# A list schedule with new latencies and port costs, helper work ranked by latest begin, and a look ahead

## The chip, the cores and the metric

The kernel runs on one core of a Trainium2 chip, as one launch. The time is device microseconds of that core. Five queues of instructions run beside each other, each in its own order: PE (TensorE, matmuls and transposes), DVE (VectorE), ACT (ScalarE), POOL (GpSimd) and SP (SyncE, which issues every DMA here). Work that isn't PE's is called helper work below.

## The reference, cut to what matters

One inference step of a two-layer backbone for 128 context tokens and 512 latent tokens, width 1024. Each layer modulates and normalises its input, projects it once for three attention mixers and for gates, runs the mixers, merges them through sigmoid gates, projects, and then runs a squared-ReLU MLP of width 4096.

```python
for l in range(DEPTH):                      # 2 layers; context and latent tokens alike
    sh1, sc1, g1, sh2, sc2, g2 = split(silu(c) @ w_mod[l] + b_mod[l], 6)
    h = rmsnorm(x, g_pre_mix) * (1 + sc1) + sh1
    qa, ka, va, qbd, kvbd, kbr, qc, kc, vc, gates = split(h @ w_in)
    oa = windowed attention with a sink      # 8 heads of 64, 2 key heads, axial rotary
    ob = latent attention                    # 8 heads, low-rank queries and keys
    oc = attention with normalised q and k   # 8 heads of 64, 2 key heads, axial rotary
    ga, gb, gc = split(sigmoid(gates), 3)
    mixed = (ga * (oa @ w_oa) + gb * (ob @ w_ob) + gc * (oc @ w_oc)) @ w_out
    x = x + g1 * rmsnorm(mixed, g_post_mix)
    h = rmsnorm(x, g_pre_mlp) * (1 + sc2) + sh2
    x = x + g2 * rmsnorm(square(relu(h @ w_mlp1)) @ w_mlp2, g_post_mlp)
```

It returns both outputs and the new keys and values of the context tokens.

## The kernel before

**Precision.** Every float32 operand of a matmul is split in two parts: ACT copies it rounded (`wh`, `ah`, `oh`, `ph`), DVE subtracts that from the original (`wl`, `al`, `ol`, `pl`). `mm3` (line 507) then runs three matmuls in place of one. So each weight costs one DMA into a raw buffer `wr` (three in turn), ACT and DVE work, and three times its matmuls.

**Stages of a layer.** All 640 tokens go through together, in five tiles of 128. First come the projections and the heads of mixer B (`b_proj`, `b_rope`, `b_heads`), then the groups of heads of mixers A and C (`gqa_group`), 100 to 634 us in layer 0 and 1262 to 1803 us in layer 1. For each block of 128 queries PE makes the scores (`sps`), DVE their negative maximum (`nm`), ACT the exponentials (`pt`), DVE the reciprocal of the sum (`rc`), POOL multiplies (`pt`, `normalise`, line 920). PE turns them (`tps`), ACT and DVE split them (`ph`, `pl`), PE multiplies by the values (`ops`). `drive` (line 1808) mixes fill work into these loops: the gates' matmuls (`gate_gen`) and, in layer 0, the modulation vectors (`mod_gen`, line 648), which use DVE, ACT and POOL to add up weighted rows of `w_mod` in `macc`.

Then `merge` (line 1525) loads the heads' outputs back (`orw`), splits them (`oh`, `ol`), multiplies, and scales by the gates (`tg`); `wout` projects into `fps`, and `post` and `norm_mod` add the residual and normalise. The MLP's first half starts with `mlp1_first`, then `sums` (line 1663) makes sums of the inputs (`t0` to `t3`, split in `t0h`, `t0l` and so on), and `mlp1_pair` (line 1698) runs 14 pairs of blocks a layer with seven products in place of eight; POOL makes four sums `s` of the weights `wq` for each pair. The second half is `mlp2_block` and, last, `kblock`.

**The order of the work.** None of these functions issues anything. `Recorder.record` (line 223) notes each operation with what it depends on, `cost` (line 188) guesses how long it holds its engine (`busy`) and when its result is there (`wait`), and `buffers` adds nodes for buffers that are taken and given back. `schedule` (line 335) then runs a list schedule: it always takes the engine that can begin first, and on it the operation with the lowest `prio` of those ready, where `prio` is the place in the program. `emit` issues the operations in the order in which the schedule began them; that is each engine's order on the chip. In `schedule` a result is seen by another engine 0.2 us after its end (`LAT`, line 169), by PE 0.35 us after (`LAT_PE`, line 170); a DVE operation without PSUM operands that begins while any POOL operation runs takes up to 0.6 of the overlap longer; a POOL operation is never slowed; PE always has its full clock. Since `emit` issues everything, the profile puts nearly all instructions at line 461; they are told apart by the tiles that they write and read.

Of the kernel before, what the change touches and what calls it, by code (L numbers as in the profile page):

```python
# [29 lines left out]
QB_SCALE = 96.0 ** -0.5  # L30
LAT = 512

# [118 lines left out]


class Op:
    __slots__ = ("eng", "name", "args", "kw", "prio", "busy", "wait", "preds", "succs", "left", "ready", "start", "end", "dma", "views", "sb", "tokens", "ring")


class Queue:
# [7 lines left out]
class Recorder:  # L165

    LAT = 0.2
    LAT_PE = 0.35  # L170

    def __init__(self, nc):
        self.nc = nc
# [49 lines left out]
    def record(self, eng, name, args, kw):  # L223
        op = Op()
        op.eng, op.name, op.args, op.kw = eng, name, args, kw
        op.prio = len(self.ops) - self.offset
        op.dma = name == "dma_start"
        op.preds, op.succs, op.views, op.tokens, op.ring = {}, [], [], 0, None
        everything = list(enumerate(args)) + list(kw.items())
        outs = [v for k, v in everything if isinstance(v, View) and k in (0, "out", "accum_out")]  # L230
        ins = [v for k, v in everything if isinstance(v, View) and k not in (0, "out", "accum_out")]
        op.views = outs + ins
        op.sb = not any(v.root.space == "PSUM" for v in op.views)
        op.busy, op.wait = self.cost(op, outs, ins)
        if op.dma:
            v = op.views[0]
            op.wait = (v.hi - v.lo) * v.idx.size * 4
        for views, write in ((ins, False), (outs, True)):
            for v in views:
                r, m, keep, seen = v.root, v.mask(), [], False  # L240
                for a in r.acc:
                    o, w, lo, hi, am = a
                    if o is not op and (write or w) and am & m and lo < v.hi and v.lo < hi:
                        seen = True
                        raw = w and not write
                        self.edge(op, o, raw)
# [12 lines left out]
        return op  # L259
# [7 lines left out]
    def node(self):  # L267
        op = Op()
        op.eng, op.preds, op.succs, op.busy, op.wait, op.dma, op.prio, op.views = None, {}, [], 0, 0, False, 0, []
        op.tokens, op.ring = 0, None  # L270
        return op


# [59 lines left out]


    def schedule(self):
        everything = self.ops + self.buffers()
        for o in everything:
            o.left, o.ready = len(o.preds) + o.tokens, 0.0
            for p, data in o.preds.items():
                p.succs.append((o, data))  # L340
        engines = ("tensor", "vector", "scalar", "gpsimd", "sync")
        free = dict.fromkeys(engines, 0.0)
        later = {e: [] for e in engines}
        now = {e: [] for e in engines}
        count = 0
        pool_end, net = 0.0, 0.0

        def less(s, t, todo):
            nonlocal count
            s.ready = max(s.ready, t)  # L350
            s.left -= 1
            if not s.left:
                if s.eng is None:
                    s.start = s.end = s.ready
                    todo.append(s)
                else:
                    count += 1
                    heapq.heappush(later[s.eng], (s.ready, count, s))

        def release(o):  # L360
            todo = [o]
            while todo:
                p = todo.pop()
                if p.ring:
                    takes, bufs, given = p.ring
                    given[0] += 1
                    if bufs + given[0] <= len(takes):
                        less(takes[bufs + given[0] - 1], p.end, todo)
                for s, data in p.succs:
                    if s.eng is None:  # L370
                        t = p.end if data else p.start
                    elif not data:
                        t = p.start
                    elif p.eng is None or p.eng != s.eng or p.dma:
                        t = p.end + (self.LAT_PE if s.eng == "tensor" else self.LAT)
                    else:
                        t = p.end
                    less(s, t, todo)

        free_nodes = [o for o in everything if not o.left]  # L380
        for o in free_nodes:
            o.start = o.end = 0.0
            if o.eng is None:
                release(o)
            else:
                count += 1
                heapq.heappush(later[o.eng], (0.0, count, o))
        order = []
        while True:
            best = None  # L390
            for e in engines:
                if now[e]:
                    t = free[e]
                elif later[e]:
                    t = max(free[e], later[e][0][0])
                else:
                    continue
                if best is None or t < best[0]:
                    best = (t, e)
            if best is None:  # L400
                break
            t, e = best
            while later[e] and later[e][0][0] <= t:
                _, c, o = heapq.heappop(later[e])
                heapq.heappush(now[e], (o.prio, c, o))
            o = heapq.heappop(now[e])[2]
            o.start = t
            busy, wait = o.busy, o.wait
            if o.dma:
                net = max(net, t + 1.6) + wait / 300e3  # L410
                wait = net + 0.7 - t
            elif e == "vector" and o.sb and pool_end > t:
                more = 0.6 * min(pool_end - t, busy)
                busy, wait = busy + more, wait + more
            if e == "gpsimd":
                pool_end = t + busy
            free[e] = t + busy
            o.end = t + wait
            order.append(o)
            release(o)  # L420
        assert len(order) == len(self.ops), (len(order), len(self.ops))
        return order

# [41 lines left out]
class Step:  # L465
# [290 lines left out]
    def first_norm(self, pool, xin):  # L756
# [19 lines left out]
        for n in range(2):  # L776
# [229 lines left out]
    def sm_window(self, pool, qT, kT, hh, kv, h):  # L1006
# [3 lines left out]
        for pair in ((0, 3), (1, 2)):  # L1010
# [62 lines left out]
    def prompt_group(self, pool, qT, kT, kv, sink):  # L1073
# [3 lines left out]
        for i in range(4):  # L1077
            q = qT[:, i, LAT:T]
            ov = ps[:, 0, i * P:i * P + P]
# [35 lines left out]
    def prompt_pv(self, pool, ph, pl, V, kv, oraw):  # L1115
# [5 lines left out]
        for i in range(4):  # L1121
            self.fold(pool, oraw[i // 2][:, LAT:T], o[:, i * P:i * P + P], i % 2)

# [961 lines left out]
```

## Time and profile before

| | us |
|---|---|
| median of three runs | 2422.16 |
| the three runs | 2422.16, 2417.62, 2422.25 |
| the profiled execution, its own time | 2419.41 |
| the profiled execution, span from first to last instruction | 2417.6 |

The profiled execution gives busy times for each engine and, for every instruction, its begin, its length, the idle time of its engine before it, and what ended that idle time. [...] A PE row of the timeline that has "[2.07 <-DVE kTb L461]" at its end says that PE stood still for 2.07 us until DVE had written `kTb`. The stretches are counted from the first instruction.

### The profile page before, as it was taken

How to read it: one execution, taken by the hardware profiler on the slowest of the kernel's cores; microseconds unless marked ns; L12 is line 12 of the kernel's file. 1: busy time of each engine (PE TensorE's matmuls, PEld its weight loads, DVE VectorE, ACT ScalarE, POOL GpSimd, SP SyncE). 2: the span in 40 equal slices, each digit the busy share in tenths (PEclk: the TensorE clock that was granted, in tenths of full speed). 3: DMA queues.
4: the chain of work that ended last, by engine and by line, in shares of the span. 5: the costliest groups of instructions: out<-in, count | busy, mean ns of one | idle time of the engine just before them, and what ended most of it. 6: DMA issues, size and time to landing. Idle time of an engine off the chain costs nothing. (4 is left out here: it accounts for less than half of the span.)

```text
span 2417.6 us, 39647 instructions
## 1 busy us (share of the span) xinstructions
PE 2310.5 (96%) x14303; PEld 2110.0 (87%) x14303; DVE 1686.5 (70%) x3347; ACT 1283.2 (53%) x2996; POOL 759.4 (31%) x671
## 2 busy tenths in 40 slices
PE   7998999999899899999999999999989999999998
PEld 3987899989798899987889989999989989997886
DVE  3689588887474798888865684776756569895444
ACT  4577556666433565654544674655643355555222
POOL 1335233442032375343521121232212317540001
PEclk9999999999899999999999999999999999999999
DMA  6353323333563454476634322222236534446432
GB/s 245 109 145 109 111 75 107 110 98 103 168 201 110 144 177 140 146 244 223 199 110 104 78 68 82 62 69 69 75 110 196 167 131 156 146 131 198 134 109 86
DMA packets 252453, 317.12 MB, mean 131 GB/s; under 512 B 37328, under 2 KB 169696, under 8 KB 251744
## 3 DMA queue, kind: packets, MB, share of 16 engines
q1 hardware_dynamic: 252256, 314.58, 41.6%
q8 instruction: 113, 1.85, 0.3%
q14 instruction: 84, 0.69, 0.1%
HBM read 251.84 MB, written 57.44 MB: 128 GB/s over the span
## 5 line engine op out<-in xcount | busy, mean ns | idle before, releaser
L461 DVE TENSOR_TENSOR wl<-wr,wh 128x256 fp32r<-128x256 f32 (+5 forms) x768 | 362.7, 512 | 190.1 <-ACT wh L461 184.6
L461 ACT ACTIVATE wh<-wr 128x256 fp32r<-128x256 f32 (+5 forms) x768 | 280.0, 423 | 298.8 <-PE lps L461 137.4
L461 POOL TENSOR_SCALAR pt<-pt,rc 128x640 f32<-128x640 f32 (+1 forms) x192 | 156.7, 822 | 397.8 <-DVE rc L461 312.9
L461 PE MATMUL lps<-wh,ah 128*128 128x512 f32 x640 | 254.4, 397 | 1.9 <-ACT ah L461 1.9
L461 PE MATMUL lps<-wh,al 128*128 128x512 f32 x640 | 253.2, 396 | 0.1
L461 PE MATMUL lps<-wl,ah 128*128 128x512 f32 x640 | 252.1, 394 | 0.0
L461 POOL TENSOR_TENSOR rs<-ss,mhalf 128x1 f32<-128x1 f32 x60 | 37.7, 634 | 470.5 <-DVE ss L461 465.4
L461 POOL TENSOR_TENSOR macc<-macc,mr 128x512 f32<-128x512 f32 x84 | 129.1, 1537 | 163.2 <-ACT mr L461 132.6
L461 ACT ACTIVATE pt<-sps,nm 128x640 f32<-128x640 f32 (+2 forms) x192 | 142.0, 742 | 62.9 <-DVE nm L461 51.3
L461 DVE TENSOR_TENSOR pl<-tps,ph 128x512 fp32r<-128x512 f32 (+2 forms) x240 | 147.8, 630 | 30.2 <-ACT ph L461 28.6
L461 PE MATMUL sps<-h2h,wh 128*128 128x320 f32 (+2 forms) x464 | 146.6, 316 | 8.5 <-DVE f L461 7.6
L461 PE MATMUL sps<-h2h,wl 128*128 128x320 f32 (+2 forms) x464 | 146.0, 315 | 3.7 <-DVE wl L461 3.7
L461 PE MATMUL tps<-ident,pt 128*128 128x128 f32 x896 | 142.3, 275 | 5.2 <-POOL pt L461 3.7
L461 PEld LDWEIGHTS lps<-wh,ah 128*128 128x128 f32 x640 | 120.6, 188 | 30.2 <-ACT ah L461 2.3
L461 PEld LDWEIGHTS lps<-wl,ah 128*128 128x128 f32 x640 | 120.5, 188 | 28.8 <-issue 1.0
L461 PE MATMUL sps<-h2l,wh 128*128 128x320 f32 (+2 forms) x464 | 145.3, 313 | 0.0
L461 PEld LDWEIGHTS lps<-wh,al 128*128 128x128 f32 x640 | 120.5, 188 | 28.1 <-DVE al L461 0.6
L461 ACT ACTIVATE ph<-tps 128x512 fp32r<-128x512 f32 (+2 forms) x240 | 128.7, 555 | 22.6 <-PE tps L461 18.8
L461 ACT ACTIVATE r<-r 128x640 f32<-128x640 f32 (+1 forms) x120 | 84.0, 711 | 102.2 <-DVE r L461 101.0
L461 PE MATMUL sps<-oh,wh 128*128 128x320 f32 x384 | 121.8, 320 | 16.5 <-ACT oh L461 16.4
L461 POOL TENSOR_TENSOR s<-wq 128x512 f32<-128x512 f32 x56 | 96.3, 1728 | 129.9 <-DMA wq<-in_w_mlp 100.8
L461 DVE TENSOR_TENSOR wl<-s,wh 128x512 fp32r<-128x512 f32 x112 | 126.1, 1144 | 7.0 <-ACT wh L461 7.0
(335 smaller groups left out, 7399.2 us busy)
## 6 DMA issues: line engine op xcount, KB each, us to landing
wr<-in_w_in SPq DMA_DIRECT2D x72, 512.0 KB, 3.9
wr<-in_w_mlp SPq DMA_DIRECT2D x72, 512.0 KB, 4.2
wq<-in_w_mlp SPq DMA_DIRECT2D x56, 512.0 KB, 5.4
mr<-in_w_mod SPq DMA_DIRECT2D x48, 512.0 KB, 4.6
ar<-a SPq DMA_DIRECT2D x56, 320.0 KB, 4.7
wr<-in_w_mod SPq DMA_DIRECT2D x32, 512.0 KB, 3.9
th<-th SPq DMA_DIRECT2D x96, 160.0 KB, 1.8
tg<-th SPq DMA_DIRECT2D x48, 320.0 KB, 3.5
```

What stands on the lines that cost most here:

```text
L461: getattr(getattr(self.nc, o.eng), o.name)(*args, **kw)
```

## The change

Only the recorder's schedule changes; no operation is added, removed or resized. The schedule now runs eight times (`PASSES`) and the order with the earliest modelled end is issued.

- **Latencies.** One `LAT` of 0.06 us from any engine to any other, PE included, in place of 0.2 and 0.35.
- **Port.** A POOL operation counts as a rival of DVE only if it is a `tensor_tensor` of more than 4 elements a row (`op.both`). A DVE operation without PSUM operands beside it runs at 0.38 of its speed while both run (before: 1 / 1.6, beside any POOL operation); the POOL operation is charged 1.2 times its cost.
- **PE's clock.** After more than 2.6 us of idle time PE is charged double for 3.4 us, after more than 4 us for 6.8 us.
- **Rank.** The first pass ranks by program order as before. After each pass `latest` goes back over what was scheduled and finds for every operation the latest begin that would leave the end where it is, with PE's order of that pass and the buffers' handing on as further edges. In the passes that follow, every operation that isn't PE's (DMA issues too) is ranked by it. PE keeps its program order among what is ready.
- **Look ahead.** From the second pass on, when DVE, ACT or POOL would begin an operation and another is going to be ready before that one would end, and its rank is over 10 us earlier (`URGENT`), the engine takes a ready operation that fits before it, or else waits for it.

```diff
-    LAT = 0.2
-    LAT_PE = 0.35
+    LAT = 0.06
+    URGENT = 10.0
+    PASSES = 8
...
+        op.time = op.busy, op.wait
+        op.both = eng == "gpsimd" and name == "tensor_tensor" and outs[0].idx.size > 4
...
     def schedule(self):
...
+        best = None
+        for o in everything:
+            o.rank = o.prio
+        for i in range(self.PASSES):
+            order = self.one(everything, i > 0)
+            end = max(o.end for o in order)
+            if best is None or end < best[0]:
+                best = end, order
+            self.latest(everything, end)
+            for o in self.ops:
+                if o.eng != "tensor":
+                    o.rank = o.late
+        return best[1]
+
+    def latest(self, everything, end):
+
+        for o in everything:
+            o.late = end
+        before, gave = {}, {}
+        last = None
+        for o in self.done:
+            if o.eng == "tensor":
+                before[o], last = last, o
+        for p, t in self.given:
+            gave.setdefault(t, []).append(p)
+        for o in reversed(self.done):
+            for p, data in o.preds.items():
+                t = o.late
+                if data:
+                    t -= p.end - p.start
+                    if o.eng is not None and p.eng != o.eng:
+                        t -= self.LAT
+                p.late = min(p.late, t)
+            for p in gave.get(o, ()):
+                p.late = min(p.late, o.late)
+            p = before.get(o)
+            if p is not None:
+                p.late = min(p.late, o.late - p.busy)
...
-                    elif p.eng is None or p.eng != s.eng or p.dma:
-                        t = p.end + (self.LAT_PE if s.eng == "tensor" else self.LAT)
-                    else:
-                        t = p.end
+                    t = p.end if data else p.start
+                    if data and s.eng is not None and (p.eng != s.eng or p.dma):
+                        t += self.LAT
...
-                heapq.heappush(now[e], (o.prio, c, o))
-            o = heapq.heappop(now[e])[2]
+                heapq.heappush(ready, (o.rank, c, o))
+            if look and soon and e in ("vector", "scalar", "gpsimd"):
+
+                come = [r for r, c, u in heapq.nsmallest(6, soon) if r < t + ready[0][2].busy and u.rank < ready[0][0] - self.URGENT]
+                if come:
+                    fit = [q for q in ready if t + q[2].busy <= come[0] + 0.03]
+                    if not fit:
+                        free[e] = come[0]
+                        continue
+                    q = min(fit)
+                    ready.remove(q)
+                    heapq.heapify(ready)
+                    heapq.heappush(ready, (-1e9, q[1], q[2]))
+            o = heapq.heappop(ready)[2]
...
             elif e == "vector" and o.sb and pool_end > t:
-                more = 0.6 * min(pool_end - t, busy)
+                more = 0.62 * min(pool_end - t, busy / 0.38)
                 busy, wait = busy + more, wait + more
-            if e == "gpsimd":
+            elif o.both:
+                busy, wait = 1.2 * busy, 1.2 * wait
                 pool_end = t + busy
+            elif e == "tensor":
+                if t - free[e] > 2.6:
+                    half = t + (6.8 if t - free[e] > 4 else 3.4)
+                if t < half:
+                    busy, wait = 2 * busy, wait + busy
```

## Rows read from the trace of the kernel before

**Rows 1.** Page: each engine's busy time, share of the span and instructions.
```profile
PE 2310.5 (96%) x14303; PEld 2110.0 (87%) x14303; DVE 1686.5 (70%) x3347; ACT 1283.2 (53%) x2996; POOL 759.4 (31%) x671
```

**Rows 2.** Stretches: length, busy time (instructions) by engine, PEclk, DMA share, GB/s.
```profile
0.00:100.00 100.00, 85.58 (x432) 58.88 (x433) 42.23 (x133) 49.14 (x112) 15.22 (x26) 0.97 0.55 183
100.00:634.00 534.00, 508.46 (x3547) 476.88 (x3546) 416.00 (x928) 335.75 (x824) 201.76 (x207) 0.99 0.37 108
634.00:660.00 26.00, 17.42 (x82) 16.41 (x83) 12.07 (x20) 9.87 (x19) 0.00 (x0) 0.74 0.73 243
786.00:1262.00 476.00, 460.80 (x2559) 413.82 (x2558) 386.29 (x592) 263.78 (x536) 215.74 (x142) 0.99 0.53 173
1262.00:1803.00 541.00, 527.65 (x3757) 504.69 (x3756) 366.90 (x923) 320.78 (x830) 122.47 (x162) 1.00 0.28 78
1803.00:1830.00 27.00, 18.88 (x98) 17.59 (x97) 13.34 (x21) 10.23 (x20) 1.12 (x1) 0.81 0.74 250
1961.00:2190.00 229.00, 216.11 (x1413) 210.97 (x1414) 194.32 (x278) 132.59 (x253) 117.52 (x72) 0.98 0.46 148
2406.00:2417.60 11.60, 3.27 (x15) 2.29 (x13) 6.70 (x11) 1.45 (x4) 1.10 (x2) 0.74 0.56 188
```

**Rows 3.** Timeline near 185: start, length, engine, operation, count, idle before it.
```profile
184.21 1.22 DVE L461 SCALAR_TENSOR_TENSOR macc<-wr,scT,macc 128x512 f32<-128x512 f32 x1
185.46 1.93 DVE L461 TENSOR_TENSOR kTb<-sps,kTb 64x768 fp32r<-64x768 f32 x2
...
187.53 0.53 PE L461 MATMUL sps<-kTb,qd 128*128 128x320 f32 x2 [2.07 <-DVE kTb L461]
```

**Rows 4.** Timeline near 255.
```profile
254.05 0.19 ACT L461 ACTIVATION_READ_ACCUMULATOR pt<-sps,nm 128x1 f32 x1
...
254.17 1.57 DVE L461 TENSOR_TENSOR wl<-wr,wh 128x512 fp32r<-128x512 f32 x1
...
257.25 0.33 PE L461 MATMUL tps<-ident,pt 128*128 128x128 f32 x1 [2.31 <-POOL pt L461]
```

**Rows 5.** Two shorter stretches, columns as in rows 2.
```profile
186.00:194.00 8.00, 6.30 (x33) 5.77 (x33) 7.32 (x13) 4.93 (x12) 4.96 (x5) 0.79 0.29 85
...
826.00:840.00 14.00, 10.09 (x53) 9.55 (x52) 11.88 (x10) 8.36 (x18) 11.33 (x8) 0.76 0.31 94
```

**Rows 6.** Timeline near 640, where the merge begins.
```profile
637.94 0.74 ACT L461 ACTIVATE oh<-orw 128x640 fp32r<-128x640 f32 x1 [2.45 <-DMA orw<-o]
...
638.73 0.90 PE L461 MATMUL sps<-oh,wh 128*128 128x320 f32 x2 [4.79 <-ACT oh L461]
...
639.62 10.84 SPq L461 DMA_DIRECT2D orw<-o  x6
...
647.76 0.90 PE L461 MATMUL sps<-oh,wh 128*128 128x320 f32 x2 [3.83 <-ACT oh L461]
```

**Rows 7.** Timeline near 793, from the output projection to the MLP.
```profile
792.72 0.55 POOL L461 TENSOR_TENSOR rs<-ss,mhalf 128x1 f32<-128x1 f32 x1 [5.55 <-DVE ss L461]
...
794.03 1.40 DVE L461 SCALAR_TENSOR_TENSOR f<-fps,rs,gg 128x512 f32<-128x512 f32 x2
...
795.58 0.42 PE L461 MATMUL sps<-h2h,wh 128*128 128x384 f32 x1 [3.81 <-DVE f L461]
```

**Rows 8.** Timeline near 825, where the first pair of MLP blocks begins.
```profile
820.58 6.95 POOL L461 TENSOR_TENSOR s<-wq 128x512 f32<-128x512 f32 x2 [20.53 <-DMA wq<-in_w_mlp]
...
828.12 3.26 DVE L461 TENSOR_TENSOR t3l<-hfull,t3h 128x640 fp32r<-128x640 f32 x2 [2.99 <-ACT t3h L461]
...
830.38 0.42 PE L461 MATMUL sps<-t1h,wh 128*128 128x320 f32 x1 [2.05 <-ACT wh L461]
...
833.11 0.64 PE L461 MATMUL sps<-h2h,wl 128*128 128x320 f32 x1 [1.87 <-DVE wl L461]
```

**Rows 9.** Tile s: count, then shortest, median and longest ns, first and last begin.
```profile
L461 DVE TENSOR_TENSOR wl<-s,wh x112: 674/992/1791, 833.0 to 2173.1; 128x512 fp32r<-128x512 f32 x112
L461 POOL TENSOR_TENSOR s<-wq x56: 1285/1644/5758, 820.6 to 2154.2; 128x512 f32<-128x512 f32 x56
```

More of the change, by code (lines that the diff above doesn't have):

```diff
@@ L153 @@
 class Op:
-    __slots__ = ("eng", "name", "args", "kw", "prio", "busy", "wait", "preds", "succs", "left", "ready", "start", "end", "dma", "views", "sb", "tokens", "ring")
+    __slots__ = ("eng", "name", "args", "kw", "prio", "busy", "wait", "preds", "succs", "left", "ready", "start", "end", "dma", "views", "sb", "tokens", "ring",
+                 "rank", "late", "time", "both")
 class Queue:
@@ L269, in node @@
         op.eng, op.preds, op.succs, op.busy, op.wait, op.dma, op.prio, op.views = None, {}, [], 0, 0, False, 0, []
-        op.tokens, op.ring = 0, None
+        op.tokens, op.ring, op.time, op.both = 0, None, (0, 0), False
         return op
@@ L337, in schedule, with one @@
         for o in everything:
-            o.left, o.ready = len(o.preds) + o.tokens, 0.0
             for p, data in o.preds.items():
                 p.succs.append((o, data))
+        best = None
[34 more added lines that the diff above has]
+                p.late = min(p.late, o.late - p.busy)
+    def one(self, everything, look):
         engines = ("tensor", "vector", "scalar", "gpsimd", "sync")
@@ L344, in schedule @@
         now = {e: [] for e in engines}
+        order, self.done, self.given = [], [], []
         count = 0
-        pool_end, net = 0.0, 0.0
+        pool_end, net, half = 0.0, 0.0, 0.0
         def less(s, t, todo):
@@ L352, in less, with arrive, release @@
             if not s.left:
-                if s.eng is None:
-                    s.start = s.end = s.ready
-                    todo.append(s)
-                else:
[L357 to L361, printed above, removed]
+                arrive(s, todo)
+        def arrive(s, todo):
+            nonlocal count
+            if s.eng is None:
+                s.start = s.end = s.ready
+                self.done.append(s)
+                todo.append(s)
+            else:
+                count += 1
+                heapq.heappush(later[s.eng], (s.ready, count, s))
+        def release(todo):
             while todo:
@@ L367, in release @@
                     if bufs + given[0] <= len(takes):
-                        less(takes[bufs + given[0] - 1], p.end, todo)
+                        t = takes[bufs + given[0] - 1]
+                        self.given.append((p, t))
+                        less(t, p.end, todo)
                 for s, data in p.succs:
[L370 to L373, printed above, removed]
-                    elif p.eng is None or p.eng != s.eng or p.dma:
-                        t = p.end + (self.LAT_PE if s.eng == "tensor" else self.LAT)
-                    else:
-                        t = p.end
-                    less(s, t, todo)
[L380 to L388, printed above, removed]
+                    t = p.end if data else p.start
+                    if data and s.eng is not None and (p.eng != s.eng or p.dma):
+                        t += self.LAT
+                    less(s, t, todo)
+        for o in everything:
+            o.left, o.ready = len(o.preds) + o.tokens, 0.0
+            if o.ring:
+                o.ring[2][0] = 0
+        for o in [o for o in everything if not o.left]:
+            todo = []
+            arrive(o, todo)
+            release(todo)
         while True:
@@ L402, in schedule @@
             t, e = best
-            while later[e] and later[e][0][0] <= t:
-                _, c, o = heapq.heappop(later[e])
-                heapq.heappush(now[e], (o.prio, c, o))
-            o = heapq.heappop(now[e])[2]
+            ready, soon = now[e], later[e]
+            while soon and soon[0][0] <= t:
+                _, c, o = heapq.heappop(soon)
+                heapq.heappush(ready, (o.rank, c, o))
[11 more added lines that the diff above has]
+            o = heapq.heappop(ready)[2]
             o.start = t
-            busy, wait = o.busy, o.wait
+            busy, wait = o.time
             if o.dma:
@@ L412, in schedule @@
             elif e == "vector" and o.sb and pool_end > t:
-                more = 0.6 * min(pool_end - t, busy)
+                more = 0.62 * min(pool_end - t, busy / 0.38)
                 busy, wait = busy + more, wait + more
-            if e == "gpsimd":
+            elif o.both:
+                busy, wait = 1.2 * busy, 1.2 * wait
                 pool_end = t + busy
+            elif e == "tensor":
[3 more added lines that the diff above has]
+                    busy, wait = 2 * busy, wait + busy
             free[e] = t + busy
-            o.end = t + wait
+            o.busy, o.end = busy, t + wait
             order.append(o)
-            release(o)
+            self.done.append(o)
+            release([o])
         assert len(order) == len(self.ops), (len(order), len(self.ops))
```

## The prediction, made before the changed kernel ran

> **What bounds the kernel now.** I read the page's busy times first. PE is busy 2310.5 of 2417.6 us, the next engine, DVE, 1686.5 [rows 1]. The change adds, removes and resizes nothing, so PE's 14303 matmuls stay, and all it can win is time in which PE stands still or runs at half its clock: 2417.6 - 2310.5 = 107.1 us idle, and the granted clock.
>
> Second, the stretches by stage, to see where those 107 us lie: length less PE's busy time [rows 2]. The begin has 14.4, the two attention stages 25.5 and 13.4, the begins of the two merges 8.6 and 8.1, 786 to 1262 (MLP of layer 0 up to the next layer) 15.2, 1961 to 2190 (first half of the MLP of layer 1) 12.9, the tail 8.3. That is 106.4; three quiet stretches hold the rest. So there is no single hole: most of it is many short stalls beside helpers that are themselves 50 to 85% busy (DVE 416 of 534 us in the first attention stage, 194 of 229 in 1961 to 2190).
>
> Third, the timeline around long stalls, to ask of each whether the helper was late because it did something less pressing, or because its own inputs were late. Only the first kind is in reach of another order.
>
> **Stalls that are out of reach.** At the begin PE waits for the first loads and norms: 14.4. The merge's first product waits 4.79 us for `oh`, the next one 3.83 [rows 6]: SP holds the six loads `orw` for 10.84 us while the stretch moves 243 GB/s, and their three buffers and the pool they lie in come free only as the attention ends. SP's rank changes too, but its queue has nothing else to let pass: it issues what is ready, and PE wants these loads as soon as they can land. Two merges, 8.6 + 8.1 = 16.7. The tail is the last norm, 8.3. From the output projection to the MLP PE waits 3.81 for `f`, since the new PSUM banks are those that `f` reads [rows 7]; the row repeats once, at 1964. Of it only the order is wrong: POOL's `rs` ends at 792.72 + 0.55 = 793.27, `f` begins at 794.03, since DVE had another operation ahead that waited. 0.76 each, two times 1.5 in reach, 6.1 not. Together 14.4 + 16.7 + 8.3 + 6.1 = 45.5.
>
> **Stalls in reach.** 25.5 + 13.4 + 15.2 + 12.9 - 2 x 3.81 = 59.4, and the 1.5 above.
>
> *Rank by latest begin.* Near 185 DVE runs `macc`, fill work that nobody waits for, for 1.22 us ahead of the `kTb` that PE waits 2.07 us for [rows 3]. Program order put it first; by latest begin it goes behind. `kTb` then comes 1.22 earlier, 59% of the stall. Near 255 the exponentials' sums are there at 254.05 + 0.19 = 254.24, but DVE takes a weight split of 1.57 us first, up to 255.74, and PE waits 2.31 for `pt` [rows 4]: 1.50 of it, 65%. Near 828 DVE first waits 2.99 for `t3h` and then splits `t3l`, an input of one of the pair's last products, for 3.26 us; the split `wl` that PE needs first is behind it, and PE waits 1.87 [rows 8]. That order goes right altogether. The 2.05 just before it is another case: PE waits for `wh`, whose source `s` POOL made in 6.95 us for two additions [rows 8]. The same pair of stalls stands once more, at 1999 (2.31) and 2002 (1.87).
>
> So a stall of this kind gives back some 60% to all of itself. These three are only 2.07 + 2.31 + 1.87 = 6.25 of the 59.4 us, and no row here says how much of the rest is of this kind and how much lies within one chain. Bounds: 0 and 59.4. I take half, 29.7: the three give more than half, and an order can only shorten a stall as far as the work ahead of it was less pressing.
>
> *Clock.* Long stalls cost twice: 186 to 194 has a granted clock of 0.79, so 8 x 0.21 = 1.7 us at the lower of the two levels, and 826 to 840 lost 14 x 0.24 = 3.4 [rows 5]. With 1.7 for 255 and for 2000 (an estimate from the first) that is 8.5 in reach. It follows the stalls: half, 4.3; bounds 0 and 8.5.
>
> *Latencies.* The trace has `oh` done at 638.68 and PE begins at 638.73 [rows 6]: 0.05, where the old schedule had 0.35 and the new one has 0.06. No instruction gets faster; the orders fit the chip better, and a spare is gone (a rival below). Costed at nothing by itself; bounds the same as the rival's.
>
> *Port.* DVE's `wl<-s` takes 0.67 alone and up to 1.79; POOL's `s` takes 1.29 at least, 1.64 in the middle and once 5.76 [rows 9]. The new charge, DVE at 0.38 of its speed, gives 0.67 / 0.38 = 1.77, which the row bears out; POOL's 1.2 gives 1.55, near the middle and far from 5.76. That longest one falls where DVE runs splits of two SBUF inputs without a pause. [...]
>
> *Look ahead and SP.* An engine idles at most for as long as the operation that it holds back, and only for one over 10 us more pressing; DVE has 118 us without work in the first attention stage [rows 2], so I cost it at nothing; without such cover, each one holds up what is queued behind on that engine by up to its length (1.2 to 1.6 us in rows 3 and 4). DMA issues move with their rank, but SP mostly waits for buffers, and a load goes when its buffer is free.
>
> **Sum.** 29.7 + 4.3 + 1.5 = 35.5. The profiled execution took 2419.41, 2.75 below the median of 2422.16. 2419.4 - 35.5 = 2383.9, and with 2.75 for the median 2387. All in reach: 59.4 + 8.5 + 1.5 = 69.4, so 2353.
>
> **The rivals.**
>
> *All of it (0.13).* The eight passes remove nearly every stall that isn't set by data: 2353, with 2338 to 2362 about it. For it: the three long ones that I followed were all wrong orders. Against: DVE is 85% busy from 1961 to 2190, and the wait for `wh` at 830 is a chain through POOL.
>
> *The gain is eaten, or the order hardly moves (0.18).* The old latencies were a spare: ACT, DVE and PE in turn were charged 0.2 + 0.35 for two hops that take about 0.1. With 0.06 PE is sent to a product as the model has it ready, and whatever is later on the chip is a stall. There are 24 heads a layer with five turned blocks each, 240 chains `tps`, `ph`, `pl`, `ops`; at 0.15 us each they cost 36 us and the gain is gone: 2422. The same time comes out if no pass beats the first, in program order. For it: 25.5 us of idle time over the first attention stage's 3547 matmuls shows that stalls are many and short today. Against: the fill work gives PE other products to run in these loops. Of the 0.18, 0.08 is still faster (down to 2410), 0.08 the same, 0.02 slower.
>
> *POOL starves (0.14, slower).* Place: the 28 pairs of MLP blocks. DVE, ranked by latest begin, runs its SBUF splits back to back, POOL's sums stretch as in the one of 5.76 us, and PE waits 2.05 for `wh` as at 830 [rows 8, 9]. Two pairs have that already; 26 x 2.05 = 53 on top of the forecast is 2440. It outweighs the gain from 35.5 / 2.05 = 17 pairs on. Against: the new ranks know the chain through `s` and would start it earlier, and the median `s` is 1.64. [...]
>
> *Forecast (0.55).* 2387, with 2362 to 2410: from a quarter to nearly all of what is in reach.
>
> **How the numbers follow.** The time is the forecast's, 2387. About 0.2%, some 5 us, is what a measurement of this kernel can tell from no change. Faster by more than that: 0.55 + 0.13 + 0.08 = 0.76. Within it 0.08. Slower 0.14 + 0.02 = 0.16. The range goes from 2346, in the lower half of "all of it" (about 0.06 lies below), to 2428, which takes in the eaten gain and leaves out nearly all of the starved POOL (0.13).
>
> **What would show it.** Right: the counts of [rows 1] unchanged; PE's idle time from 100 to 634 down from 25.5 to about 13, in the second attention stage from 13.4 to about 7; the merges still near 8 each; `macc` behind `kTb`, `t3l` behind the first `wl`; `f` right after `rs`. Wrong: idle time in the merges or at the begin falls (then I misjudged what sets them); the attention stages have as many stalls but others; `s` well above a median of 1.64 and PE waiting for `wh` in many pairs; or PE's idle time falls and the span doesn't, which would mean that the page hides stalls within a busy PE.

## The result and the profile after

The changed kernel takes 2394.82 us, median (2388.71 to 2397.34), 0.9888 [0.9866, 0.9910] of the kernel before it on the same chip (2422.06): 1.1% faster. The profiled executions took 2388.71 and 2419.41, so the two traces differ by 30.7 us (the medians by 27.2), and every difference below is between these two. One execution of the experiments below, of e3, was slow (2824.79 us at a granted clock of 0.746, where the others of e3 have 0.987), and e3's figures leave it out.

The page of after: the span and the busy times, which answer [rows 1].

```profile
span 2386.9 us, 39558 instructions
...
PE 2296.2 (96%) x14303; PEld 2101.0 (88%) x14303; DVE 1703.2 (71%) x3347; ACT 1294.2 (54%) x2996; POOL 767.6 (32%) x671
```

The counts are those of before. PE's idle time went from 107.1 to 2386.9 - 2296.2 = 90.7, so 16.4 of the 30.7 us are idle time. The other 14.3 are time in which PE counts as busy.

The stretches of after, which answer [rows 2] in the same order and with the same columns (PEclk is the share of TensorE's full clock that was granted); each bound is moved by as much as the first product of its stage has moved.

```profile
0.00:96.70 96.70, 85.87 (x426) 57.63 (x427) 42.43 (x133) 49.24 (x112) 15.03 (x26) 0.98 0.57 187
96.70:617.30 520.60, 500.13 (x3553) 473.15 (x3551) 411.25 (x928) 337.49 (x824) 213.02 (x207) 1.00 0.38 111
617.30:643.40 26.10, 17.08 (x81) 16.07 (x82) 12.55 (x21) 11.08 (x20) 0.17 (x1) 0.74 0.74 251
768.40:1243.40 475.00, 460.30 (x2573) 413.75 (x2572) 399.97 (x590) 266.77 (x532) 210.07 (x142) 0.99 0.53 173
1243.40:1781.80 538.40, 527.07 (x3745) 502.76 (x3744) 365.97 (x924) 323.08 (x832) 127.37 (x163) 1.00 0.28 78
1781.80:1808.80 27.00, 19.85 (x95) 17.71 (x94) 12.99 (x21) 10.90 (x20) 1.45 (x1) 0.75 0.77 250
1939.10:2163.30 224.20, 215.36 (x1428) 212.09 (x1427) 198.17 (x280) 137.00 (x258) 115.03 (x72) 0.98 0.47 153
2375.30:2386.90 11.60, 3.20 (x14) 2.25 (x12) 6.56 (x11) 1.45 (x4) 1.10 (x2) 0.75 0.54 187
```

Length less PE's busy time gives the idle time, before and after: begin 14.4 and 10.8, first attention stage 25.5 and 20.5, first merge 8.6 and 9.0, MLP of layer 0 15.2 and 14.7, second attention stage 13.4 and 11.3, second merge 8.1 and 7.2, first half of the MLP of layer 1 12.9 and 8.8, tail 8.3 and 8.4. No stage lost most of its idle time.

What PE waited for, before and then after: total us, times, longest.

```profile
PE nps L461 <- POOL xn L461: 10.1, 2, 5.3
PE sps L461 <- DVE f L461: 7.6, 2, 3.8
PE sps L461 <- DVE kTb L461: 6.1, 6, 2.1
PE sps L461 <- DVE r L461: 5.9, 6, 1.7
PE sps L461 <- ACT wh L461: 4.4, 2, 2.3
...
PE sps L461 <- DVE wl L461: 3.7, 2, 1.9
...
PE rowps L461 <- DMA wr<-in_c_ctx: 2.8, 1, 2.8
```

```profile
PE sps L526 <- ACT oh L526: 16.2, 4, 4.9
PE sps L526 <- DVE wl L526: 12.1, 2, 6.3
PE sps L526 <- DVE f L526: 6.2, 2, 3.1
PE rowps L526 <- DMA wr<-in_c_ctx: 6.1, 1, 6.1
...
PE nps L526 <- POOL xn L526: 2.9, 1, 2.9
...
PE mps L526 <- DVE macc L526: 2.3, 1, 2.3
...
PE sps L526 <- DVE kTb L526: 0.5, 1, 0.5
```

The waits for `kTb`, for `r` and for `wh` are nearly gone, and that for `xn` has fallen from 10.1 to 2.9. But the wait for the split `wl` has grown from 3.7 to 12.1, and it is now two waits of some 6 us; `rowps` waits 3.3 us more for a load, and a new wait for `macc` has come.

The lengths of the stages show more than the idle times. I worked them out from the traces: a stage ends where PE begins the first product of the next one, a first pair where PE begins the first product with `t1h`. The first column is before, in us; the others are changes to it, for after and for some of the experiments below; each column is one execution.

```
                            before  after     e2     e3     e8     e6     e5    e11
begin, projections 0         127.9   -3.3   -0.4   -4.0   +1.4   -0.1   -4.1   -0.7
first heads 0                122.6   -5.0   -2.0   -5.1   -5.5   -6.6   -5.7   +2.4
attention 0                  388.1   -8.3   -1.3   -8.9   -1.2   -7.2   -8.2   +1.0
merge, output 0              156.8   -0.9   -1.4   -1.0   -2.8   -1.8   -1.4   -0.4
MLP 0, first pair             34.8   +6.1   -2.3   +9.0   -0.5   +5.6   +0.4   -3.7
MLP 0, other pairs           182.3  -11.6   -2.8  -11.6  -10.0  -11.6  -11.6   -1.5
MLP 0, second half           239.9   +4.4   +1.5   +5.5   +0.7   +3.1   +3.9   +1.1
projections, first heads 1   196.4   +0.4   +7.9   +2.2   +1.9   +1.9   +1.2   +1.1
attention 1                  359.4   -3.0   +1.1   -2.4   +0.4   -3.2   -3.0   +1.6
merge, output 1              155.9   -0.7   +0.3   -1.0   -0.5   -0.3   -1.2   +0.6
MLP 1, first pair             34.8   +5.3   -0.5   +9.2   -0.5   +6.0   -1.2   -3.8
MLP 1, other pairs           180.7  -10.1   -2.3  -10.1   -8.5  -10.1  -10.1   +0.6
MLP 1, second half, tail     237.8   -4.1   -3.2   -2.0   -2.6   -3.9   -4.1   +0.4
sum                         2417.6  -30.8   -5.4  -20.1  -27.6  -28.0  -45.0   -1.3
```

The rows of the first pairs don't hold the same work in every column. PE comes to the product with `t1h` at different points of its work: after 214 matmuls before, 224 in after, e3, e8, e6 and e5, 204 in e2 and e11. Before, the wait of 1.87 for `wl` [rows 8] and ten products behind it lie in the row below. Only the two rows of a layer together hold the same 1392 (layer 0) and 1380 (layer 1) matmuls in every column:

```
both rows             after     e2     e3     e8     e6     e5    e11
MLP 0, all pairs       -5.5   -5.1   -2.6  -10.5   -6.0  -11.2   -5.2
MLP 1, all pairs       -4.8   -2.8   -0.9   -9.0   -4.1  -11.3   -3.2
```

In after, the pairs of the MLP gave 5.5 + 4.8 = 10.3, and the first heads of layer 0 and the two attention stages 5.0 + 8.3 + 3.0 = 16.3. The second half of the first MLP took 4.4 of that back. Within the pairs all idle time is now in one wait in each first pair: 6.35 and 5.75 us, where PE waited 2.05 + 1.87 and 2.31 + 1.87 before. The pairs behind it have none.

This is the place of the wait of 6.35, in the trace of after: DVE, then POOL, then PE at the first pair of layer 0 (start, length, engine, operation, idle before it).

```profile
802.24 0.82 DVE L526 TENSOR_TENSOR t1l<-hfull,t1h 128x640 fp32r<-128x640 f32 x1
802.98 1.92 DVE L526 TENSOR_TENSOR t0l<-hfull,t0h 128x640 fp32r<-128x640 f32 x1
804.82 1.92 DVE L526 TENSOR_TENSOR t2l<-hfull,t2h 128x640 fp32r<-128x640 f32 x1
806.66 1.90 DVE L526 TENSOR_TENSOR t0l<-hfull,t0h 128x640 fp32r<-128x640 f32 x1
808.48 1.75 DVE L526 TENSOR_TENSOR wl<-wq,wh 128x512 fp32r<-128x512 f32 x1
810.15 1.88 DVE L526 TENSOR_TENSOR hfull<-hfull 128x640 f32<-128x640 f32 x1
811.95 1.75 DVE L526 TENSOR_TENSOR wl<-wq,wh 128x512 fp32r<-128x512 f32 x1
```

```profile
802.90 1.31 POOL L526 TENSOR_TENSOR s<-wq 128x512 f32<-128x512 f32 x1 [20.63 <-DMA wq<-in_w_mlp]
804.29 1.76 POOL L526 TENSOR_TENSOR s<-s,wq 128x512 f32<-128x512 f32 x1
806.01 1.86 POOL L526 TENSOR_TENSOR s<-wq 128x512 f32<-128x512 f32 x1
807.84 1.84 POOL L526 TENSOR_TENSOR s<-wq,s 128x512 f32<-128x512 f32 x1
809.64 1.70 POOL L526 TENSOR_TENSOR s<-wq 128x512 f32<-128x512 f32 x1
811.43 1.73 POOL L526 TENSOR_TENSOR s<-s,wq 128x512 f32<-128x512 f32 x1
```

```profile
813.76 0.64 PE L526 MATMUL sps<-h2h,wl 128*128 128x320 f32 x1 [6.35 <-DVE wl L526]
```

DVE's split `t1l` takes 0.82. From 802.90 POOL makes its sums `s`, one behind the other, and from there on each operation of DVE takes 1.75 to 1.92. PE stands for 6.35 us until the second `wl` is done. The same wait stands at 1977.16 in layer 1, with 5.75.

### The profile page after: what moved, and what is told of

It reads as the page before. It is cut to its first block, busy times and chain, and to the rows that moved or that the text cites. A ratio compares the mean times of both kernels' runs of the same rounds, so it can differ in the third digit from the quotient of the medians.

```text
span 2386.9 us, 39558 instructions
## 1 busy us (share of the span) xinstructions
PE 2296.2 (96%) x14303; PEld 2101.0 (88%) x14303; DVE 1703.2 (71%) x3347; ACT 1294.2 (54%) x2996; POOL 767.6 (32%) x671
## 5 line engine op out<-in xcount | busy, mean ns | idle before, releaser
L526 DVE TENSOR_TENSOR wl<-wr,wh 128x256 fp32r<-128x256 f32 (+5 forms) x768 | 380.4, 543 | 151.5 <-ACT wh L526 147.0
L526 POOL TENSOR_SCALAR pt<-pt,rc 128x640 f32<-128x640 f32 (+1 forms) x192 | 168.8, 887 | 361.9 <-DVE rc L526 310.4
L526 PE MATMUL sps<-h2h,wl 128*128 128x320 f32 (+2 forms) x464 | 145.3, 313 | 12.1 <-DVE wl L526 12.1
L526 POOL TENSOR_TENSOR s<-wq 128x512 f32<-128x512 f32 x56 | 90.2, 1611 | 134.6 <-DMA wq<-in_w_mlp 102.3
L526 PE MATMUL sps<-ol,wh 128*128 128x320 f32 x384 | 122.8, 321 | 0.0
```

The lines of the kernel that those rows point to most:

```text
L526: getattr(getattr(self.nc, o.eng), o.name)(*args, **kw)
```

## The experiments

Three questions: which part of the change made the gain (my theory: the rank by latest begin; rivals: the new costs; the look ahead), what makes PE wait some 6 us at each first pair (DVE and POOL slowing each other, or the wrong rank), and whether SP's rank matters. Ratios are to the kernel before on the same chip, with 95% intervals. The first four shared one chip and its runs of before, so did e5 to e8, and e9 to e12.

**e1, the new latencies alone**, on the kernel before:

```diff
-    LAT = 0.2
-    LAT_PE = 0.35
+    LAT = 0.06
+    LAT_PE = 0.06
```

> The kernel before with one edit: both latencies of the schedule are 0.06 us, the rest of its costs and its program-order rank as they were. Theory (the gain is the rank's; a latency by itself makes no operation faster): 2422, within 5 us of before. Rival (the gain is the fit of the latencies, PE is no longer kept from products that are ready): 2405 or less, over half of the 27 us. Second rival (the old latencies were a spare): over 2430.

Measured 2426.72, 1.0020 [1.0007, 1.0033]. The latencies by themselves bring no gain, rather 0.2% of loss. If that is the rival "the old latencies were a spare", it is small: some 5 us, not the 36 that I had priced it at. What makes the loss no run shows.

**e2, all new costs, one pass in program order**, on after:

```diff
-    PASSES = 8
+    PASSES = 1
```

> The changed kernel with one pass: new latencies, new port costs and PE's clock in the schedule, but rank by program order and no look ahead. Theory (rank): 2415 to 2424. Rival (the new costs alone let the list schedule place helper work better): 2400 or less. The stalls near the first pair of MLP blocks (2.05 and 1.87 us of PE before) stay as they were by the theory, since program order makes them.

Measured 2412.03, 0.9967 [0.9954, 0.9981]. The costs alone give 0.3%. In the tables its attention stages hardly move (-1.3 and +1.1). Its pairs give 7.9 in all, and the projections and first heads of layer 1 lose as much.

**e3, rank and look ahead with the old costs**, on after: the latencies, the port's charge and PE's clock as before.

```diff
-    LAT = 0.06
+    LAT = 0.2
+    LAT_PE = 0.35
...
-                more = 0.62 * min(pool_end - t, busy / 0.38)
+                more = 0.6 * min(pool_end - t, busy)
...
-            elif o.both:
-                busy, wait = 1.2 * busy, 1.2 * wait
+            if e == "gpsimd":
...
-            elif e == "tensor":
-                if t - free[e] > 2.6:
-                    half = t + (6.8 if t - free[e] > 4 else 3.4)
-                if t < half:
-                    busy, wait = 2 * busy, wait + busy
```

> The changed kernel with the costs of the kernel before (latencies 0.2 and 0.35, DVE slowed beside any POOL operation, PE always at its full clock), but with the eight passes, the rank by latest begin and the look ahead. Theory (rank): 2395 to 2402, most of the 27 us. Rival (the costs): 2415 or more. If both are needed, it lies near 2408.

Measured 2397.14, 0.9904 [0.9884, 0.9924]. So the rank, with its look ahead, brings most of the gain with the old costs too. In the first heads of layer 0 and the attention stages it is worth 5.1 + 8.9 + 2.4 = 16.4 here, as in after (16.3; e2 has 2.2), but in all pairs it gives only 3.5, where after gives 10.3. Its first pairs cost +9.0 and +9.2, beside +6.1 and +5.3 in after, but another execution of after has +9.1 and +6.1 there (e9), so that what the new port charge does for the first pairs isn't settled.

**e4, no look ahead**, on after:

```diff
-            order = self.one(everything, i > 0)
+            order = self.one(everything, False)
```

> The changed kernel without the look ahead: eight passes ranked by latest begin, new costs. Theory (rank): 2395 to 2400, like the changed kernel, since an engine seldom holds back. Rival (the look ahead keeps helpers free for pressing work and is a third of the gain or more): 2404 or more.

Measured 2398.51, 0.9913 [0.9891, 0.9936], beside 0.9888 for after: 0.25%, with intervals that overlap. Beside the second measurement of after, 0.9869 (e9), it is 0.44%, with intervals that don't. So the look ahead is small here, and whether it is worth anything isn't settled.

**e5, the sums of the first two pairs of each layer on DVE**, on after. The edit changes nothing but the engine of 16 of the 112 sums; the schedule is worked out anew with it. At the first pairs POOL has no sum to make.

```diff
-        tt = nc.gpsimd.tensor_tensor
+        tt = (nc.vector if n <= 6 else nc.gpsimd).tensor_tensor
```

> The changed kernel with the weight sums of the first two pairs of MLP blocks of each layer on DVE in place of POOL (8 sums a layer), so that POOL adds nothing while DVE makes the splits for the first pair. Theory (at 813.8 and 1977.2 PE waits 6.35 and 5.75 us because POOL's sums slow DVE's splits from 0.82 to 1.9 us): the two waits together fall from 12.1 to 7 or less and the time to 2388 or less. Rival (the wait is the loads' landing or DVE's own queue): the waits stay at 12 or grow by the sums that DVE now makes, 2397 or more.

Measured 2377.35, 0.9809 [0.9782, 0.9837], the fastest kernel of this study, with a span of 2372.6. DVE at the same place in this kernel's trace, and two stretches there (columns as in rows 2):

```profile
803.18 0.82 DVE L526 TENSOR_TENSOR t1l<-hfull,t1h 128x640 fp32r<-128x640 f32 x1
803.92 0.82 DVE L526 TENSOR_TENSOR t2l<-hfull,t2h 128x640 fp32r<-128x640 f32 x1
804.65 0.82 DVE L526 TENSOR_TENSOR t0l<-hfull,t0h 128x640 fp32r<-128x640 f32 x1
805.39 0.69 DVE L526 TENSOR_TENSOR s<-wq 128x512 f32<-128x512 f32 x1
805.99 0.69 DVE L526 TENSOR_TENSOR wl<-wq,wh 128x512 fp32r<-128x512 f32 x1
```

```profile
782.00:811.00 29.00, 29.00 (x205) 28.97 (x205) 17.58 (x29) 16.01 (x33) 0.00 (x0) 1.00 0.35 114
811.00:820.00 9.00, 9.00 (x63) 9.00 (x63) 9.00 (x16) 4.57 (x9) 0.00 (x0) 1.00 0.54 172
```

DVE has taken over work, and still its splits end earlier, since each takes 0.82 or 0.69 again. PE is busy for all of the 38 us, and both waits of some 6 us are gone. In the table the first pairs lose 5.7 and 6.5 us against after, 12.2 of the 14.3 by which the two spans differ. So contention between DVE and POOL was the cause of the two waits. The order of DVE's work there has changed a little as well, but that isn't what removed them. In after's own order, with begins 0.73 apart behind 640 columns and 0.60 behind 512, as they are without POOL, the second `wl` would have ended at 802.98 + 4 x 0.73 + 0.60 + 0.69 = 807.19, an estimate; PE's last product ahead of the wait ended at 807.41.

**e6, SP stays in program order**, on after:

```diff
-                if o.eng != "tensor":
+                if o.eng not in ("tensor", "sync"):
```

> The changed kernel with SP ranked by program order again, all other helpers by latest begin. Theory (SP's rank brings the inputs' loads ahead of constants at the begin, and little elsewhere): PE waits near 34 us for the normalised input for 4 to 5 us as before the change, heads of mixer B begin at 127 us or later, the time is 3 to 6 us over the changed kernel: 2398 to 2401. Rival (SP's rank does nothing, the begin is set by the loads): 2395, heads begin near 124.6. Second rival (SP's rank matters in all stages): over 2405.

Measured 2390.19, 0.9865 [0.9843, 0.9887]. At the begin the 3.3 us of after are lost again (-0.1), as SP's rank would have it, and PE waits 4.83 for `xn`, as it did before (4.80), and the heads begin at 127.9. That part of the expectation holds. But in sum it costs nothing that these runs can tell, so the expected time, 2398 to 2401, fails.

**e7, the port's new charge alone**, on the kernel before:

```diff
+        op.both = eng == "gpsimd" and name == "tensor_tensor" and outs[0].idx.size > 4
...
-                more = 0.6 * min(pool_end - t, busy)
+                more = 0.62 * min(pool_end - t, busy / 0.38)
...
-            if e == "gpsimd":
+            elif o.both:
+                busy, wait = 1.2 * busy, 1.2 * wait
```

> The kernel before with the new port costs alone (only POOL's larger tensor_tensor counts, DVE at 0.38 of its speed beside it, POOL charged 1.2 times), program order, old latencies. New costs together gave 2412 and the latencies alone 2427. Theory (the port costs are the part of the new costs that helps): 2408 to 2414. Rival (parts of the costs help only together): 2418 or more.

Measured 2410.35, 0.9950 [0.9931, 0.9968]. Of the costs it is the port's that help: 0.5%, and with the new latencies and the clock added 0.3% (e2). In its trace all pairs of the MLP together give 5.8 + 4.6 = 10.4, in program order, and that is as much as after's 10.3. So, by these two traces, in the pairs the new charge does without the rank what the whole change does; the rank's own gain lies in the heads and the attention stages.

**e8, rank and look ahead for DVE alone**, on after:

```diff
-                if o.eng != "tensor":
+                if o.eng == "vector":
...
-            if look and soon and e in ("vector", "scalar", "gpsimd"):
+            if look and soon and e == "vector":
```

> The changed kernel with the rank by latest begin, and the look ahead, on DVE alone; ACT, POOL and SP by program order. Theory (the stalls that I followed were DVE's order): 2398 to 2403, most of the gain. Rival (the order of ACT, POOL and SP carries as much): 2407 or more.

Measured 2392.30, 0.9872 [0.9853, 0.9892], as fast as after. But the table shows another split: the attention stages give only 1.2 and lose 0.4, where after gave 8.3 and 3.0, and the first pairs, with the same 224 matmuls, are 6.6 and 5.8 shorter than after's. So the ranks of ACT and POOL (with their look ahead, which e8 leaves out too; e6 shows that it isn't SP's) earn some 10 us in the attention stages and give them back at the first pairs.

**e9, after once more**, without an edit, for the spread between comparisons.

> The changed kernel once more, beside the three that follow, to know what of the small differences between kernels run at other times is the chip's. Expected: 2390 to 2398. If it comes out at 2390 or less, SP by program order (2390) and the rank on DVE alone (2392) are no better than the changed kernel; if at 2395 or more, SP's rank costs some 4 us in all.

Measured 2390.68, 0.9869 [0.9854, 0.9884], beside 0.9888 the first time. The first pairs cost +9.1 and +6.1 in its trace, where after has +6.1 and +5.3 with the same kernel. The 3.0 in layer 0 are TensorE's clock, as the last section shows. Variants that are within 0.2% of each other, as e6, e8 and after, aren't told apart here.

**e10, a lower threshold for the look ahead**, on after:

```diff
-    URGENT = 10.0
+    URGENT = 7.0
```

> The changed kernel with a look ahead from 7 us of difference in rank on in place of 10, an edit that stands for no cause: another order out of the same rules. Theory (what the rules fix, such as the waits within the pairs, stays; where single operations meet moves by chance): within 6 us of the changed kernel, and the pairs without idle time again. Rival (the value 10 is what makes the gain): 2405 or more.

Measured 2395.50, 0.9891 [0.9874, 0.9908]: no gain. As expected, the pairs behind the first are again without idle time. The rows of the first pairs are +6.1 and +5.2, as in after.

**e11, the edit of e5 on the kernel before.**

> The kernel before with the weight sums of the first two pairs of each layer on DVE, all else as before. Theory (in program order DVE's wrong order, not the port alone, makes PE wait near 830 and 1999, and stalls within the pairs stay): it gains 4 to 9 us, 2412 to 2417, half or less of the 17 us that the same edit gave the changed kernel. Rival (the port is the whole cause there in either order): 2405 or less.

Measured 2415.56, 0.9971 [0.9961, 0.9981]. In the old order the same edit is worth 7 us of the median and 1.3 of the profiled execution; on after it is worth 13 at least (e5's 2377.35 beside the 2390.68 of e9) and 14.3. The pairs together gain 5.2 and 3.2, where on after the edit gains 5.7 and 6.5, and other stages give it back.

**e12, e5 and e6 together.**

> The changed kernel with both edits: weight sums of the first two pairs of each layer on DVE, and SP by program order. Theory (SP's rank gave 3.3 us at the begin and gave them back near the first pairs, where earlier weights let POOL's sums begin beside DVE's splits; with the sums on DVE that cost is gone): no better than the sums on DVE alone, 2377 to 2382. Rival (SP's rank costs in other stages): 2373 or less.

Measured 2380.03, 0.9820 [0.9801, 0.9839]; with e5's 0.9809 the same. SP's rank is worth nothing that can be told, with or without the sums on DVE.

## Why the prediction was right, point by point

The forecast of 2387 lies 8 us below the 2394.82 of the first comparison and 4 below the 2390.68 of the second; faster by over 0.2%, as forecast. The main mechanism, the rank by latest begin, is the one that e3 and e2 show: 0.9904 without the new costs, 0.9967 without the rank. But it isn't the whole: in the pairs of the MLP the new port charge, which the forecast priced at nothing, gives as much in program order (e7, 10.4) as the change does (10.3). Several terms of the sum were off as well, and some of the errors cancel, so that the small distance of the number is in part luck.

**Half of what is in reach, 29.7.** Mis-sized. With the handovers the forecast took 31.2 us of idle time, and 16.4 went. In the attention stages I expected 25.5 to fall to 13 and 13.4 to 7; they fell to 20.5 and 11.3. Three long stalls that I had followed were no sample of the many short ones: of the 38.9 us in these stages 29.5 were stalls of 1 us or less, and 23.1 of these are left. In the other pairs of the MLP nothing is left (5.9 and 5.3 us of idle time became 0; 1.87 of each was the wait for `wl` of the first pair), more than half.

**Clock, 4.3.** Mis-sized in the other direction. The product of length and lost clock, summed over the stages of the table, went from 37.2 to 28.5, so it is 8.7 at most, about my upper bound of 8.5; some of it lies in time in which PE is idle anyway. Of the 14.3 us by which PE's busy time fell, at least 5.6 are thus not the clock. They fit the hidden first parts of stalls: a product of 320 columns has a record of 0.31 us where the next one begins 0.15 behind it, so the last record ahead of a stall covers the first part of the stall, which counts as busy. At full clock PE stood still 126 times before and 92 times after. What those places took beyond their idle time and the usual distance from begin to begin went from 23.7 to 17.7 us, an estimate from the begins in both traces. So the last of my signs of an error, stalls hidden within a busy PE, was there, though on the good side, and "idle time and the clock" was not all that the change could win.

**`macc` behind `kTb`, `f` right behind `rs`.** Right. The timeline of after at the place of [rows 3], and then at that of [rows 7]:

```profile
181.48 1.92 DVE L526 TENSOR_TENSOR kTb<-sps,kTb 64x768 fp32r<-64x768 f32 x2
...
182.93 0.56 PE L526 MATMUL sps<-kTb,qd 128*128 128x320 f32 x2 [0.17 <-ACT pt L526]
...
184.11 0.73 DVE L526 SCALAR_TENSOR_TENSOR macc<-wr,scT,macc 128x512 f32<-128x512 f32 x1
```

```profile
775.84 0.55 POOL L526 TENSOR_TENSOR rs<-ss,mhalf 128x1 f32<-128x1 f32 x1 [6.24 <-DVE ss L526]
776.42 1.41 DVE L526 SCALAR_TENSOR_TENSOR f<-fps,rs,gg 128x512 f32<-128x512 f32 x2 [0.66 <-POOL rs L526]
...
777.98 0.41 PE L526 MATMUL sps<-h2h,wh 128*128 128x384 f32 x1 [3.08 <-DVE f L526]
```

`kTb` runs first and PE's wait is no longer for it; `macc` runs 2.6 us later. `f` begins 0.03 after `rs` ends, and PE waits 3.08 in place of 3.81: 0.73 each, where the step said 0.76.

**`t3l` behind the first `wl`.** Right, and of no use: PE's waits there grew, from 2.05 + 1.87 to 6.35, though I had the second of them go altogether. I had DVE's order as the cause of [rows 8] and the order did change, but the length of the operations ahead of `wl` changed as well. In after the three splits `t0l`, `t2l`, `t0l` take 5.74 in place of 2.46, since POOL's sums run from 802.90 on, and an `hfull` stands between the two `wl` that PE needs. The forecast had this rival the wrong way round: POOL was to starve beside DVE (2440, 0.14). `s` has its median at 1.74 and its longest at 1.86, where before it had 5.76; it is DVE that lost. e5 shows it: without POOL's sums there the wait is gone. The step that failed is "the port": I costed it only by what it does to POOL. The 2.05 was misread as well. The source of that `wh` is not one of the two sums that took 6.95 us but the third, `s<-s,wq`, made from 827.61 to 828.89, behind one for a later product; and ACT made `t3h` and `r` before that `wh`, which it began at 829.71. So this wait was in part order too, POOL's and ACT's. In after, PE's clock fell with the wait for `wl`, as the stretch behind it shows:

```profile
811.00:820.00 9.00, 6.24 (x30) 6.24 (x31) 8.75 (x8) 5.17 (x11) 5.45 (x4) 0.62 0.09 29
```

With a granted clock of 0.62 (0.50 from 811.0 to 817.5 and 1.00 from 818.0 on), 0.38 x 9 = 3.4 us went at the lower of the two levels there, as much as before from 826 to 840 [rows 5].

**Out of reach.** The merges (8.6 and 8.1, now 9.0 and 7.2) and the tail (8.3, now 8.4) stayed, as said. The begin didn't: 14.4 became 10.8. "Nothing else to let pass" holds for SP's queue at the merges, not at the begin. SP's issues, of after and then of before:

```profile
15.06 0.90 SPq L526 DMA_DIRECT2D cosB<-in_k_cosB  x1
16.05 2.33 SPq L526 DMA_DIRECT2D x<-in_x_sample  x1
...
21.29 0.38 SPq L526 DMA_DIRECT2D x<-in_x_prompt  x1
```

```profile
24.01 0.43 SPq L461 DMA_DIRECT2D sink<-in_a_sink  x1
24.54 0.38 SPq L461 DMA_DIRECT2D x<-in_x_sample  x1
25.02 0.38 SPq L461 DMA_DIRECT2D x<-in_x_prompt  x1
```

Before, the last two loads of `x` stood behind all the constants, of which `sink` was the last; by latest begin they go in between, and PE waits for `xn` once, 2.89 us, in place of twice. e6 undoes it: the 3.3 us are gone. But it is worth nothing in the time (e6 with e9, e12 with e5), within what can be told.

**Latencies and look ahead, costed at nothing.** Near enough: +0.2% for the first alone (e1), 0.25 to 0.44% for the second (e4, not settled).

**New, and not foreseen:** the second half of the first MLP takes 4.4 us more, with a new wait of 2.29 for `macc` at 1119. With the fill ranked last, fill work that fits nowhere earlier may come late; e8, where it is +0.7, speaks for a rank of another engine than DVE, but e4 has +1.1, and the cause stays open.

Why the schedule, which has a charge for POOL's sums beside DVE's splits, still lets them run there is argued only: POOL has nothing else and begins a sum as soon as its four loads have landed (at 802.90 in after behind 20.63 us of idle time that ended with a load of `wq`), so its begin isn't held by the order but by when the loads come, and that on the chip differs from the model. No run tests it.

## What to carry to other kernels

Rank each helper's work by how late it may begin, not by program order: it was worth about 1% with the new costs or the old, and on DVE alone as much. Let the schedule know what two engines cost each other: that alone, in program order, was worth 0.5%. Then look in the new trace for where a stall has gathered: several of up to 2.3 us in the pairs had become one of 6 us ahead of them, and it came from two engines that slow each other (in after a split of 0.82 took up to 1.92), which the new ranks had not mended; moving a few operations off the second engine for that stretch gave another 0.6 to 0.8%. Price a stage by its length in both traces and not by PE's idle time alone, since nearly half of this gain never counted as idle time. And compare stages only where they hold the same products.

## What the runs showed of the hardware

**DVE and POOL take turns.** In the rows of after's first pair above, begins alternate one to one: `s` 802.90, `t0l` 802.98, `s` 804.29, `t2l` 804.82, `s` 806.01, `t0l` 806.66. DVE's begins lie 1.84 apart, and its own, alone, 0.73 (802.24 to 802.98). That leaves 1.11 for POOL's sum. Behind a split of 512 columns DVE's next begin is 1.67 later (808.48 to 810.15), and alone 0.60 (805.39 to 805.99 in e5), which leaves 1.07. (A sum's record alone lasts 1.29 at least.) If DVE just ran at a lower speed beside POOL, the 0.60 would become 0.60 x 1.84 / 0.73 = 1.51, not 1.67. So, by these rows, the two don't go on side by side at a lower speed, their times add up. The new charge, DVE at 0.38 of its speed and POOL at 1.2 times its cost, has both go on more slowly; by these rows the 1.70 to 1.86 of a sum is not a slower sum but one with a turn of DVE in it.

**Who gets the next turn isn't settled.** In the kernel before, one `s` took 5.76 [rows 9], at 820.58, while DVE ran without a pause up to 825.13, and ended 1.21 behind that, at 826.34; in after, with DVE as dense, none took over 1.86. No run tells what decides it.

**The clock doesn't always fall behind the same wait.** After and e9 are the same kernel. In layer 0 of both PE waits for `f`, 3.08 us up to 777.98 in after and 3.09 up to 776.49 in e9, with the same products in the 20 us up to the end of the wait and the same ones behind it. The stretch from 776 to 782, of after and then of e9 (columns as in rows 2):

```profile
776.00:782.00 6.00, 4.03 (x23) 4.06 (x24) 5.30 (x13) 4.61 (x15) 1.04 (x2) 1.00 0.73 241
```

```profile
776.00:782.00 6.00, 5.51 (x17) 5.54 (x18) 5.62 (x14) 3.13 (x10) 0.93 (x1) 0.50 0.66 248
```

The granted clock was 1.00 in after and 0.50 in e9; e5 has 0.50 at this place too, behind 3.09 us. The products of the same shape begin 0.17 apart in after and 0.32 in e9, and the first pair of layer 0 is 3.0 us longer. So a part of what a stall costs differs from one execution to the next.
